# Two transformer blocks on one core: the modulation vectors as TensorE products in four column strips

## The chip, the cores and the metric

The kernel runs on 1 core of one Trainium2 chip. The metric is the device time of one execution in microseconds (us); less is better. The engines in the text: TensorE (PE; its weight loads are shown apart as PEld), VectorE (DVE), ScalarE (ACT), GpSimd (POOL), and SyncE (SP), whose queue issues nearly all transfers.

## What is computed

Two blocks for 256 tokens of width 1024, one after the other. The first mixes four branches (forgetting attention, a linear recurrence, stick-breaking attention, attention to a memory) and ends in a feed-forward part. The second has two layers, each applied to the tokens `x` and, in the first layer, also to 256 context tokens. All is fp32. What matters here are the modulation vectors of the second block:

```python
silu_c = jax.nn.silu(c)            # 1 x 1024
silu_cc = jax.nn.silu(c_ctx)       # 1024
for l in range(2):
    mod = silu_c @ w_ada[l] + b_ada[l]                 # w_ada[l]: 1024 x 6144
    sh1, sc1, g1, sh2, sc2, g2 = jnp.split(mod, 6)
    mod_c = silu_cc @ w_ada[l][:, :n_cm * 1024] + ...  # n_cm: 6 in layer 0, 2 in layer 1
```

They need nothing but `c`, `c_ctx` and the weights (two times 24 MB), so they can be made at any time before the second block's layer uses them.

## The kernel before

**Layout.** Activations lie feature-major: 8 tiles of 128 features x 256 tokens. Nearly every projection goes by *units*: a unit is 128 x 1024 weights (512 KB) that SP brings into `raw` (5 buffers; `unit`, L442). ACT rounds it to `whi` (L357), VectorE or GpSimd makes the rest `wlo = raw - whi` (L360), and TensorE makes 24 products of 128x128 weights and 256 columns from it (`mm3`, tiles `mm`: 8 of `hh` with `whi`, 8 of `hl` with `whi`, 8 of `hh` with `wlo`). Three PSUM buffers hold `mm`, four hold everything else (`ps`, tag `at`), one holds `st`.

**Order.** A scheduling layer orders the instructions of each engine by priority, and each engine then works strictly in that order. The program is written with generators that are stepped in turn (`step`, `run`, `weave`), so that side work is spread over a stage.

**The side work of this case** is `ada_steps` (L1053). For each layer it goes over 6 groups `g` of 1024 outputs, each in 4 steps of two 128-row slices of `w_ada`: 24 steps a layer, 48 in all. A step loads 1 MB into `wada` by SP (L1071), and VectorE multiplies each slice by the column of `silu(c)` (and of `silu(c_ctx)` where `nv` is 2) and adds it to `adacc`, 128 x 1024 for each vector (L367 the first time, L363 after that): 4 instructions a step with two vectors, 2 with one. Two steps after a group's last, `ada_end` (L1095) sums over the partitions: products of `adacc` with `sel`, a 128x32 matrix with one column of ones, four to a vector, each into its own strip of 32 partitions of one PSUM bank `ad`; ACT copies the bank to `adas`; two transposes on TensorE (L1106); VectorE adds the bias (tiles `ada`).

**Where it runs.** Layer 0 (`fill0`): 12 steps are written beside stick-breaking attention and the branch after it (`take(fill, 8)`, `take(fill, 4)` in `block1`), with one buffer for `wada`, and 12 beside the first block's feed-forward part (`ffn`, L1020), one to each of its pairs of units, with two buffers. Layer 1 (`fill1`): 12 beside the context's feed-forward part of layer 0, one to two pairs, and 12 beside that of the tokens, one to a pair; two buffers. `self.fp` names pool, tag, count of buffers and the tag of `adacc`.

**The feed-forward part of the first block** has, for each of 22 pairs of units, this chain: ACT copies the gate's half out of PSUM (`gp`), VectorE makes a three-tap convolution (`cv`: one L367, two L363), ACT the silu, VectorE the product with the other half (L360, which frees the PSUM buffer), ACT `hidh`, VectorE or GpSimd `hidl`. The second block's has no convolution.

Of the kernel before, what the change touches and what calls it, by code (L numbers as in the profile page):

```python
# [10 lines left out]
F32 = mybir.dt.float32  # L11
# [3 lines left out]
AF = mybir.ActivationFunctionType  # L15
ALU = mybir.AluOpType
AX = mybir.AxisListType

P = 128
D = 1024  # L20
T = 256
KT = 8
# [299 lines left out]
class Builder:  # L322
# [339 lines left out]
    def block1(self, xt, ct, fill):  # L662
        nc = self.nc
        with self.pool("b1") as bp, self.phase("b1t", t1=4, t2=6):
            def newy():
                return tuple(Tiles([bp.tile([P, T], F32R, tag="y" + c, name="y" + c, bufs=14) for _ in range(KT)])
                             for c in "hl")
            memt = bp.tile([P, KT, T], F32, tag="acc", name="memt")
            for i in range(0, KT, 2):
                nc.sync.dma_start(memt[:, i:i + 2], self.a["tok"][1, :, i:i + 2])  # L670
            late = PV["lam"][0]
            nc.sync.dma_start(self.pv[:, :late], self.a["pv"][:, :late])
            mh = newy()
            self.rms_h(memt, "mem_g", *mh)
            mk = bp.tile([P, KT, T], F32, tag="mk", name="mk")
            mv = bp.tile([P, 2, D], F32, tag="mv", name="mv")
            kv = self.mem_kv(mh, mk, mv)
            step(kv, 1)
            nc.sync.dma_start(xt, self.a["tok"][0])
            nc.sync.dma_start(self.pv[:, late:], self.a["pv"][:, late:])  # L680
            h = self.new_h()
            self.rms_h(xt, "attn_g", *h)
            self.setup()
            self.cb = bp.tile([P, NCB], F32, tag="cb", name="cb")
            nc.sync.dma_start(self.cb, self.a["cst1"])
            wr = self.t("wfr", P)
            nc.sync.dma_start(wr, self.a["wff"].rearrange("p k c -> p (k c)"))
            self.wff = [bp.tile([P, P], F32R, tag=f"wff{q}", name=f"wff{q}") for q in "hl"]
            self.split(wr, *self.wff, eng=nc.vector)
            run(kv)  # L690
            nc.sync.dma_start(ct, self.a["tok"][2])
            acc = bp.tile([P, KT, T], F32, tag="acc", name="acc")
            ym = newy()
            run(self.mem(h, mk, mv, ym))
            self.wl = bp.tile([P, 2, KT, P], F32, tag="mk", name="wl")
            nc.sync.dma_start(self.wl, self.a["wl"])
            gf = bp.tile([P, len(LEVELS), P], F32, tag="mv", name="gf")
            nc.sync.dma_start(gf, self.a["gm"])
            nc.vector.tensor_copy(self.gm, gf)
            yl = newy()  # L700
            lru = self.lru(h, yl, bp)
            step(lru, 1)
            b3 = self.branch(3, h, ym, acc, True)
            for _ in range(8):
                step(b3, 1)
                step(lru, 1)
            run(b3, lru)
            self.fp = bp, "mk", 1, "mv"
            self.span = 12
            yf = newy()  # L710
            fox = self.fox(h, yf, bp)
            step(fox, 3)
            weave((fox, 1), (self.branch(1, h, yl, acc, False), 1))
            ys = newy()
            stick = self.stick(h, ys, bp)
            step(stick, 3)
            bf = self.branch(0, h, yf, acc, False)
            weave((stick, 3), (bf, 1), (take(fill, 8), 1))
            run(bf)
            weave((self.branch(2, h, ys, acc, False), 2), (take(fill, 4), 1))  # L720
            mx = newy()
            self.halve(acc, mx)
            for f in range(0, KT, 2):
                self.residual(xt, self.pair("out", f, mx), f)
            h = self.new_h()
            self.rms_h(xt, "ffn_g", *h, True)
            self.flush()
        with self.pool("b1f") as bp, self.phase("b1ft", t1=10, t2=6):
            def hidden(ft, pg):
                gp = bp.tile([P, 2 + T], F32, tag="gp", name="gp", bufs=3)  # L730
                nc.gpsimd.memset(gp[:, :2], 0.0)
                self.act(gp[:, 2:], pg)
                c = self.t("cv")
                w = lambda i: self.pvc("fcw", i * FT + ft)
                self.ts(c, gp[:, 0:T], w(0), self.pvc("fcb", ft), ALU.mult, ALU.add)
                self.stt(c, gp[:, 1:1 + T], w(1), c, ALU.mult, ALU.add)
                self.stt(c, gp[:, 2:2 + T], w(2), c, ALU.mult, ALU.add)
                self.act(c, c, AF.Silu)
                return c

            self.fp = bp, "wada", 2, "adacc"
            self.span = 24
            yield from self.ffn("gu", "dn", h, hidden, lambda ps, f: self.residual(xt, ps, f), bp)

# [308 lines left out]
    def ada_steps(self, l, out):  # L1053


        nc = self.nc
        raws = []
        n = 0
        for g in range(6):
            nv = 2 if l == 0 or g < 2 else 1  # L1060
            for k in range(0, KT, 2):
                if self.late:
                    self.late[0] -= 1
                    if self.late[0] == 0:
                        self.flush()
                pool, rt, nr, at = self.fp
                if k == 0:
                    acc = pool.tile([P, 2, 1024], F32, tag=at, name="adacc")
                while len(raws) < nr and n < self.span:
                    raw = pool.tile([P, 2, 1024], F32, tag=rt, name="wada", bufs=nr)  # L1070
                    nc.sync.dma_start(raw, self.a["wa"][l * 24 + n])  # L1071
                    raws.append(raw)
                    n += 1
                raw = raws.pop(0)
                with self.tc.high_priority(offset=-200):
                    for j in range(2):
                        for v in range(nv):
                            c = self.sc[:, 2 * (k + j) + v:2 * (k + j) + v + 1]
                            if k + j == 0:
                                self.ts(acc[:, v], raw[:, j], c, None, ALU.mult)  # L1080
                            else:
                                self.stt(acc[:, v], raw[:, j], c, acc[:, v], ALU.mult, ALU.add)
                if k < KT - 2:
                    yield
            self.late = [2, lambda g=g, acc=acc, nv=nv: self.ada_end(l, out, g, acc, nv)]
            yield
        self.flush()

# [3 lines left out]
            f, self.late = self.late[1], None  # L1092
            f()

    def ada_end(self, l, out, g, acc, nv):  # L1095
        nc = self.nc
        ps = self.ps("ad")
        for v in range(nv):
            for j in range(4):
                self.mm(ps[j * 32:(j + 1) * 32, :T], self.sel[:, v], acc[:, v, j * T:(j + 1) * T], start=v == 0,  # L1100
                        stop=v == nv - 1)
        s = self.cp.tile([P, T], F32, tag="adas", name="adas")
        self.act(s, ps[:, :T])
        pt = ps[:, T:]
        for b in range(2):
            nc.tensor.transpose(pt[:, b * P:(b + 1) * P], s[:, b * P:(b + 1) * P], self.cst("ident"))  # L1106
        for v in range(nv):
            src = pt.rearrange("p (b j c) -> p j b c", b=2, j=4)[:, :, :, v]
            o = PV[f"bada{l}"][0] + g * 8
            self.tt(out[v][:, g * 8:(g + 1) * 8].rearrange("p (j b) -> p j b", b=2), src,  # L1110
                    self.pv[:, o:o + 8].rearrange("p (j b) -> p j b", b=2), ALU.add)
            if g in (1, 4):
                c = out[v][:, g * 8:(g + 1) * 8]
                self.ts(c, c, 1.0, None, ALU.add)
# [386 lines left out]
    def setup(self):  # L1501
        nc, cp = self.nc, self.cp
        nc.sync.dma_start(self.cc, self.a["cst"])
        c = lambda n, w: cp.tile([P, w], F32, tag=n, name=n)
# [21 lines left out]
        for l in range(2):  # L1526
            self.ts(self.pvs(f"dw{l}"), self.pvs(f"dw{l}"), 0.5, None, ALU.mult)

        self.sc = c("sc", 16)
        self.act(self.sc, self.pvs("c"), AF.Silu)  # L1530
        self.sel = cp.tile([P, 2, 32], F32, tag="sel", name="sel")
        nc.gpsimd.memset(self.sel, 0.0)
        for v in range(2):
            nc.gpsimd.memset(self.sel[:, v, v:v + 1], 1.0)


class Tiles:
# [14 lines left out]
def program(tc, a, out, stage, order):  # L1552
    nc = tc.nc
    with ExitStack() as ctx:
        b = Builder(tc, a, ctx, order)
# [21 lines left out]
            b.mix(0, nxt[0], xt, ax0, mem, bp, bp, b.modulate(ct, ac0, 3, nxt))  # L1577
        with b.pool("h2") as h2:
            with b.pool("f0") as bp, b.phase("f0t", t1=10, t2=6):
                b.fp = bp, "wada", 2, "adacc"  # L1580
                b.span = 24
                ffn = b.layer_ffn(0, nxt[1], ct, ac0, bp)
                for i in range(12):
# [2 lines left out]
                g = b.modulate(xt, ax0, 3, nxt)  # L1586
# [47 lines left out]
```

## Time and profile before

| what | value |
|---|---|
| median of 3 runs (lowest, highest) | 3097.9 us (3092.52 to 3099.93) |
| profiled execution, its own time | 3095.87 us |
| its span, first to last instruction | 3094.1 us |
| TensorE busy | 2809.3 us (91%) |
| VectorE busy | 2152.1 us (70%) |
| ScalarE, GpSimd busy | 1344.0 us, 851.9 us |
| mean granted TensorE clock | 0.961 |

Busy time is the union of an engine's instructions. An fp32 product on TensorE shows as two matmul records, a product of rounded (fp32r) operands as one. A granted clock of 1.0 is 2.4 GHz; the other level is 1.2 GHz, and values between are means over a stretch. What ended an engine's idle time (the releaser) is inferred from semaphores.

### The profile page before, as it was taken

To read this page: it belongs to the slowest core of one execution; us is meant where nothing else is said; L and a number is where in the kernel's file an instruction comes from. 1 tells how busy PE (TensorE), PEld (TensorE's weight loads), DVE (VectorE), ACT (ScalarE), POOL (GpSimd) and SP (SyncE) were. 2 spreads that over 40 slices of the span, in tenths; PEclk is the share of its full clock that TensorE was granted. 3 is DMA by queue.
4 is the path that set the end of the run, shared out by engine and by line. 5 is a ranking of instruction groups with operands and counts; after the bars stand their busy time and mean duration, and the time that the engine had idled before them with its cause. 6 is when DMAs were issued, how large, how long until landed. Compare 5 with 4: busy or idle time off the path is not lost. (4 is left out here: it accounts for less than half of the span.)

```text
span 3094.1 us, 49653 instructions
## 1 busy us (share of the span) xinstructions
PE 2809.3 (91%) x19760; PEld 2635.7 (85%) x19760; DVE 2152.1 (70%) x3412; ACT 1344.0 (43%) x2047; POOL 851.9 (28%) x643
## 2 busy tenths in 40 slices
PE   7997889988799887898999998999999999999898
PEld 6897778888799886798899988999998888888898
DVE  7599764679974899957699348868844499321554
ACT  5474446533344544345645554445434332111443
POOL 3243322243324434542102105444520111100000
PEclk9999999998899998999999999999999999999999
DMA  5345333466547555687656986654743223344353
GB/s 201 138 164 179 114 105 132 146 214 214 192 148 266 200 190 188 214 309 284 240 206 244 333 318 235 248 202 156 281 157 123 97 96 109 120 150 153 123 179 108
DMA packets 153416, 578.18 MB, mean 187 GB/s; under 512 B 17628, under 2 KB 17756, under 8 KB 146656
## 3 DMA queue, kind: packets, MB, share of 16 engines
q1 hardware_dynamic: 152496, 574.45, 52.1%
q8 instruction: 155, 2.54, 0.3%
q10 hardware_dynamic: 688, 0.56, 0.1%
q14 instruction: 77, 0.63, 0.1%
HBM read 516.73 MB, written 58.20 MB: 186 GB/s over the span
## 5 line engine op out<-in xcount | busy, mean ns | idle before, releaser
L357 ACT ACTIVATE whi<-raw 128x1024 fp32r<-128x1024 f32 (+1 forms) x650 | 675.7, 1045 | 747.4 <-PE mm L370 397.8
L360 POOL TENSOR_TENSOR wlo<-raw,whi 128x1024 fp32r<-128x1024 f32 (+1 forms) x248 | 647.0, 2613 | 1010.3 <-ACT whi L357 721.2
L360 DVE TENSOR_TENSOR wlo<-raw,whi 128x1024 fp32r<-128x1024 f32 (+1 forms) x293 | 382.8, 1307 | 242.3 <-ACT whi L357 231.0
L370 PE MATMUL mm<-hh,whi 128*128 128x256 f32 x3184 | 485.7, 294 | 33.1 <-DVE cv L360 19.2
L370 PE MATMUL mm<-hh,wlo 128*128 128x256 f32 x3184 | 469.3, 290 | 19.7 <-DVE wlo L360 17.6
L370 PE MATMUL mm<-hl,whi 128*128 128x256 f32 x3184 | 475.3, 292 | 0.0
L370 PEld LDWEIGHTS mm<-hh,whi 128*128 128x128 f32 x3184 | 431.2, 198 | 46.8 <-DVE cv L360 20.9
L370 PEld LDWEIGHTS mm<-hh,wlo 128*128 128x128 f32 x3184 | 426.0, 197 | 23.2 <-DVE wlo L360 18.8
L370 PEld LDWEIGHTS mm<-hl,whi 128*128 128x128 f32 x3184 | 431.7, 200 | 4.3 <-issue 3.6
L363 DVE SCALAR_TENSOR_TENSOR ca<-yp,pv,ca 128x256 f32<-128x256 f32 x720 | 357.2, 557 | 2.2
L370 PE MATMUL mm<-h,raw 128*128 128x256 f32 x1184 | 267.1, 379 | 0.0
L370 PEld LDWEIGHTS mm<-h,raw 128*128 128x128 f32 x1184 | 222.7, 190 | 29.5 <-issue 0.4
L363 DVE SCALAR_TENSOR_TENSOR adacc<-wada,sc,adacc 128x1024 f32<-128x1024 f32 x140 | 229.9, 1659 | 7.2 <-DMA wada<-in_wa 6.8
L360 POOL TENSOR_TENSOR gF<-cum 128x128 f32<-128x128 f32 x192 | 98.2, 542 | 337.2 <-DVE cum L1192 171.3
L370 PE MATMUL mm<-yh,whi 128*128 128x256 f32 x896 | 139.7, 295 | 23.1 <-ACT yh L357 16.3
L370 PEld LDWEIGHTS mm<-yh,whi 128*128 128x128 f32 x896 | 122.6, 199 | 30.1 <-ACT yh L357 20.6
L363 DVE SCALAR_TENSOR_TENSOR gt<-gt,mm 128x256 f32<-128x256 f32 x72 | 29.9, 416 | 161.7 <-ACT gt L357 161.6
L370 PE MATMUL mm<-yh,wlo 128*128 128x256 f32 x896 | 133.2, 290 | 2.8 <-DVE wlo L360 2.8
L370 PE MATMUL mm<-yl,whi 128*128 128x256 f32 x896 | 133.0, 290 | 2.6 <-DVE yl L363 2.1
L370 PEld LDWEIGHTS mm<-yh,wlo 128*128 128x128 f32 x896 | 120.0, 197 | 4.4 <-DVE wlo L360 3.2
L370 PEld LDWEIGHTS mm<-yl,whi 128*128 128x128 f32 x896 | 120.2, 197 | 3.6 <-DVE yl L363 2.7
L370 PE MATMUL mm<-y,raw 128*128 128x256 f32 x512 | 116.5, 384 | 0.0
(289 smaller groups left out, 4069.2 us busy)
## 6 DMA issues: line engine op xcount, KB each, us to landing
raw<-in_ws SPq DMA_DIRECT2D x744, 512.0 KB, 3.8
lo<-wlo SPq DMA_DIRECT2D x109, 512.0 KB, 3.0
wlo<-lo SPq DMA_DIRECT2D x109, 512.0 KB, 3.6
wada<-in_wa SPq DMA_DIRECT2D x48, 1024.0 KB, 4.9
raw<-in_ws SPq DMA_DIRECT2D x32, 384.0 KB, 3.0
memt<-in_tok SPq DMA_DIRECT2D x4, 256.0 KB, 4.6
xt<-in_tok SPq DMA_DIRECT2D x1, 1024.0 KB, 6.8
ct<-in_tok SPq DMA_DIRECT2D x1, 1024.0 KB
```

What stands on the lines that cost most here:

```text
L357: return self.nc.scalar.activation(out, in_, f, **k)
L360: return (eng or self.nc.vector).tensor_tensor(out=out, in0=a, in1=b, op=op)
L363: return self.nc.vector.scalar_tensor_tensor(out=out, in0=a, scalar=s, in1=b, op0=op0, op1=op1)
L370: return self.nc.tensor.matmul(out, lhsT=l, rhs=r, start=start, stop=stop, **k)
```

## The change

The products of a step are made on TensorE. `sc` becomes eight 128x32 matrices, one for each slice, with `silu(c)` and `silu(c_ctx)` in the first two columns and zeros in the others. Each step issues 8 products: for each of its two slices four, one to a strip of 32 partitions of the bank `ad`, with 256 columns of `wada` each. The bank is taken at a group's first step and accumulates over its 4 steps. `ada_end` no longer multiplies by `sel`; it starts at the copy to `adas` and comes one step after the group's last, not two. `adacc` and `sel` go, `wada` has three buffers instead of two in the feed-forward parts, and the lowered priority of the side work goes with the VectorE instructions.

```diff
-            self.fp = bp, "mk", 1, "mv"
+            self.fp = bp, "mk", 1
...
-            self.fp = bp, "wada", 2, "adacc"
+            self.fp = bp, "wada", 3
...
-                pool, rt, nr, at = self.fp
+                pool, rt, nr = self.fp
                 if k == 0:
-                    acc = pool.tile([P, 2, 1024], F32, tag=at, name="adacc")
+                    ps = self.ps("ad")
                 while len(raws) < nr and n < self.span:
...
-                with self.tc.high_priority(offset=-200):
-                    for j in range(2):
-                        for v in range(nv):
-                            c = self.sc[:, 2 * (k + j) + v:2 * (k + j) + v + 1]
-                            if k + j == 0:
-                                self.ts(acc[:, v], raw[:, j], c, None, ALU.mult)
-                            else:
-                                self.stt(acc[:, v], raw[:, j], c, acc[:, v], ALU.mult, ALU.add)
+                for j in range(2):
+                    for q in range(4):
+                        self.mm(ps[q * 32:(q + 1) * 32, :T], self.sc[:, k + j], raw[:, j, q * T:(q + 1) * T],
+                                start=k + j == 0, stop=k + j == KT - 1)
...
-            self.late = [2, lambda g=g, acc=acc, nv=nv: self.ada_end(l, out, g, acc, nv)]
+            self.late = [1, lambda g=g, ps=ps, nv=nv: self.ada_end(l, out, g, ps, nv)]
...
-    def ada_end(self, l, out, g, acc, nv):
+    def ada_end(self, l, out, g, ps, nv):
         nc = self.nc
-        ps = self.ps("ad")
-        for v in range(nv):
-            for j in range(4):
-                self.mm(ps[j * 32:(j + 1) * 32, :T], self.sel[:, v], acc[:, v, j * T:(j + 1) * T], start=v == 0,
-                        stop=v == nv - 1)
-        s = self.cp.tile([P, T], F32, tag="adas", name="adas")
+        s = self.t("adas")
         self.act(s, ps[:, :T])
...
-        self.sc = c("sc", 16)
-        self.act(self.sc, self.pvs("c"), AF.Silu)
-        self.sel = cp.tile([P, 2, 32], F32, tag="sel", name="sel")
-        nc.gpsimd.memset(self.sel, 0.0)
-        for v in range(2):
-            nc.gpsimd.memset(self.sel[:, v, v:v + 1], 1.0)
+        self.sc = cp.tile([P, KT, 32], F32, tag="sc", name="sc")
+        nc.gpsimd.memset(self.sc, 0.0)
+        self.act(self.sc[:, :, :2], self.pvs("c").rearrange("p (k v) -> p k v", v=2), AF.Silu)
```

**What moves, on VectorE, in the first block's feed-forward part** (`cv`, `hidl`, `wlo` are its own work; `adacc` the side work). Before, between two convolutions:

```order
L367 TENSOR_SCALAR cv<-gp,pv 128x256
L363 SCALAR_TENSOR_TENSOR adacc<-wada,sc,adacc 128x1024
L360 TENSOR_TENSOR wlo<-raw,whi 128x1024
L363 SCALAR_TENSOR_TENSOR cv<-gp,pv,cv 128x256
L363 SCALAR_TENSOR_TENSOR adacc<-wada,sc,adacc 128x1024
L363 SCALAR_TENSOR_TENSOR cv<-gp,pv,cv 128x256
L363 SCALAR_TENSOR_TENSOR adacc<-wada,sc,adacc 128x1024
L360 TENSOR_TENSOR cv<-cv,mm 128x256
L363 SCALAR_TENSOR_TENSOR adacc<-wada,sc,adacc 128x1024
```

Now:

```order
L367 TENSOR_SCALAR cv<-gp,pv 128x256
L363 SCALAR_TENSOR_TENSOR cv<-gp,pv,cv 128x256 x2
L360 TENSOR_TENSOR cv<-cv,mm 128x256
L360 TENSOR_TENSOR hidl<-cv,hidh 128x256
L360 TENSOR_TENSOR wlo<-raw,whi 128x1024
```

The side work is gone from between the steps of a pair's chain.

**On TensorE, in the same part, at the end of a group of the side work.** Before (`ad<-cc,adas` are the transposes):

```order
L370 MATMUL mm<-hh,wlo 128x256 x8
L370 MATMUL ad<-adacc,sel 32x256 x4
L370 MATMUL mm<-hh,whi 128x256 x8
L370 MATMUL mm<-hl,whi 128x256 x8
L370 MATMUL mm<-hh,wlo 128x256 x8
L370 MATMUL mm<-hh,whi 128x256
L370 MATMUL ad<-adacc,sel 32x256 x4
L370 MATMUL mm<-hh,whi 128x256 x5
L1106 MATMUL ad<-cc,adas 128x128 x2
```

Now:

```order
L370 MATMUL mm<-hh,wlo 128x256 x8
L370 MATMUL ad<-wada,sc 32x256 x5
L1099 MATMUL ad<-cc,adas 128x128 x2
L370 MATMUL ad<-wada,sc 32x256 x3
L370 MATMUL mm<-hh,whi 128x256 x8
```

Eight strip products stand after every pair of units, and the transposes of the group before stand inside the eight of the next step.

**On TensorE, beside stick-breaking attention** (`z` its logits, `av` its values), the first step of the side work now:

```order
L370 MATMUL z<-se,cb 128x256
L370 MATMUL z<-se,cb 128x128 x2
L370 MATMUL mm<-hh,whi 128x256 x4
L370 MATMUL mm<-hl,whi 128x256 x2
L370 MATMUL av<-sw,av 64x256
L370 MATMUL ad<-wada,sc 32x256
L370 MATMUL av<-sw,av 64x256
L370 MATMUL av<-sw,av 64x128 x2
L370 MATMUL ad<-wada,sc 32x256 x7
```

The first 12 steps now stand on TensorE here and in the branch after it. In the trace of before five of them ran on VectorE during the forgetting attention ahead of this stage, from 236 us on.

## Rows read from the trace of the kernel before

**Rows 1.** The page: busy time and share of the span by engine.

```profile
PE 2809.3 (91%) x19760; PEld 2635.7 (85%) x19760; DVE 2152.1 (70%) x3412; ACT 1344.0 (43%) x2047; POOL 851.9 (28%) x643
```

**Rows 2.** Groups of instructions: form xcount | busy us, mean ns | idle before, releaser.

```profile
L363 DVE SCALAR_TENSOR_TENSOR adacc<-wada,sc,adacc 128x1024 f32<-128x1024 f32 x140 | 229.9, 1659 | 7.2 <-DMA wada<-in_wa 6.8
...
L370 PE MATMUL ad<-adacc,sel 128*32 128x256 f32 x160 | 13.8, 443 | 10.5 <-DVE adacc L363 10.5
L370 PE MATMUL mm<-h,raw 128*128 128x256 f32 x1184 | 267.1, 379 | 0.0
```

**Rows 3.** Busy time by stretch: length, PE, PEld, DVE, ACT, POOL, PEclk, DMA share, GB/s.

```profile
576.00:696.00 120.00, 106.15 (x791) 97.41 (x790) 93.18 (x100) 51.29 (x74) 42.68 (x19) 0.91 0.55 195
696.00:873.00 177.00, 149.91 (x1105) 142.88 (x1106) 165.50 (x191) 68.82 (x115) 67.82 (x44) 0.88 0.54 192
1886.00:2040.00 154.00, 147.15 (x1178) 144.54 (x1179) 120.55 (x105) 62.54 (x91) 76.74 (x36) 0.95 0.67 242
2140.00:2230.00 90.00, 85.25 (x700) 83.33 (x699) 74.12 (x71) 41.96 (x68) 43.74 (x21) 0.96 0.68 249
```

**Rows 4.** Stretches, PE and PEld alone: length, PE, PEld, PEclk, DMA share, GB/s.

```profile
853.00:873.00 20.00, 20.00 (x169) 20.00 (x168) 1.00 0.35 127
1710.00:1752.00 42.00, 42.00 (x352) 42.00 (x351) 1.00 0.90 327
```

**Rows 5.** Stretch 696 to 873, adacc alone: length, PE, PEld, DVE, PEclk, DMA, GB/s.

```profile
696.00:873.00 177.00, 4.76 (x48) 1.13 (x48) 69.02 (x48) 0.88 0.54 192
```

**Rows 6.** Waits of PE, 696 to 873: total us, times, longest us.

```profile
PE mm L370 <- DVE cv L360: 13.9, 6, 3.8
PE ad L370 <- DVE adacc L363: 6.7, 3, 5.3
```

**Rows 7.** Timeline of PE around strip products: start us, us, instruction, xcount.

```profile
1941.30 1.12 PE L370 MATMUL mm<-hh,wlo 128*128 128x256 f32 x8
1942.35 1.07 PE L370 MATMUL ad<-adacc,sel 128*32 128x256 f32 x16
1943.35 0.98 PE L370 MATMUL mm<-hh,whi 128*128 128x256 f32 x6
...
1944.16 0.39 PE L1106 MATMUL ad<-cc,adas 128*128 128x128 f32 x2
```

**Rows 8.** Timeline of DVE behind the last adacc of that feed-forward part.

```profile
863.27 2.37 DVE L367 TENSOR_SCALAR cv<-gp,pv 128x256 f32<-128x256 f32 x1
...
869.65 2.44 DVE L367 TENSOR_SCALAR cv<-gp,pv 128x256 f32<-128x256 f32 x1
```

**Rows 9.** Waits of PE, 576 to 696.

```profile
PE mm L370 <- ACT yh L357: 4.1, 2, 2.9
PE ad L370 <- DVE adacc L363: 3.7, 1, 3.7
```

**Rows 10.** Waits of PE, 228 to 310, beside the forgetting attention.

```profile
PE pt L942 <- DVE fs L367: 3.7, 3, 1.8
```

**Rows 11.** Waits of PE, 873 to 930.

```profile
PE st L370 <- DVE fsum L566: 5.0, 1, 5.0
```

**Rows 12.** Waits of PE, 1886 to 2040.

```profile
PE mm L370 <- DVE hidl L360: 2.8, 1, 2.8
PE mm L370 <- DVE wlo L360: 2.2, 2, 1.9
```

**Rows 13.** Timeline of PE, the tokens' feed-forward part: in brackets idle before, releaser.

```profile
2190.11 0.64 PE L370 MATMUL ad<-adacc,sel 128*32 128x256 f32 x8
2190.68 0.74 PE L370 MATMUL mm<-hh,whi 128*128 128x256 f32 x4
2196.16 0.69 PE L1106 MATMUL ad<-cc,adas 128*128 128x128 f32 x2 [4.75 <-ACT adas L357]
```

**Rows 14.** Timeline of ACT ahead of the copy of that bank.

```profile
2194.51 1.06 ACT L357 ACTIVATE whi<-raw 128x1024 fp32r<-128x1024 f32 x1 [6.53 <-DMA raw<-in_ws]
...
2195.73 0.38 ACT L357 ACTIVATE adas<-ad 128x256 f32<-128x256 f32 x1
```

More of the change, by code (lines that the diff above doesn't have):

```diff
@@ L1579, in program @@
             with b.pool("f0") as bp, b.phase("f0t", t1=10, t2=6):
-                b.fp = bp, "wada", 2, "adacc"
+                b.fp = bp, "wada", 3
                 b.span = 24
```

## The prediction

> **What bounds the kernel now.** I read the page's table of engines first: the reader is to see TensorE at 91% of the span and VectorE at 70% [rows 1]. Over the whole program TensorE is the bound, so a change that adds products to it should cost. But a share of the span averages over stages, so next I read the stretches in which the side work runs [rows 3]. The feed-forward part of the first block, 696 to 873 us, stands out: VectorE is busy for 165.5 of its 177 us, TensorE for 149.9, and the granted TensorE clock is 0.88. There VectorE is the bound. In the other three stretches TensorE leads, with 106 of 120, 147 of 154 and 85 of 90 us. A granted clock of 0.88, if it is a mixture of the two levels 1.2 and 2.4 GHz, means that 24% of the stretch ran at 1.2, some 42 us, and half of these, 21 us, is what this costs.
>
> Third come the waits of TensorE in that stretch [rows 6]: 13.9 us for `cv`, the convolution's last product on VectorE, and 6.7 for `adacc`. Last I looked for a stretch in which TensorE does the same work without stalls: 853 to 873 us, behind the last of the side work, has 169 products in 20.00 us at clock 1.00 [rows 4], so 0.1183 us a product. What the stage would be without stalls can be worked out from that.
>
> **What the change removes.** VectorE loses 140 instructions of 1659 ns, 229.9 us [rows 2], and 20 lighter ones that begin a group; 69.0 us of these lie in 696 to 873 us [rows 5]. TensorE loses 80 products with `sel` (160 records), in 8 visits to the strips of 8 products and 4 of 4.
>
> **What it adds: the price of a step.** An fp32 product on the full array takes two records of 379 ns that overlap: 267.1 us for 592 products, 0.45 us each [rows 2]. In strips it is cheaper: 16 records, 8 products, start at 1942.35 us and the next work at 1943.35, so 1.00 us for eight [rows 7]; 8 records take 0.57 (2190.11 to 2190.68) [rows 13]. So four strips do four products in about the time of one on the whole array. Around a visit something is lost: the 8 products ahead take 1.05 us where eight take 0.96 elsewhere (853 to 873: 8 x 0.118 = 0.95), and the 6 behind 0.81 (1943.35 to 1944.16) where 0.72 is due [rows 4, 7], 0.09 on either side. A visit of 8 then costs 1.00 + 0.18, about 1.2 us, one of 4 about 0.76. The change has 48 visits of 8: 57.6 us, against 8 x 1.2 + 4 x 0.76 = 12.6 removed. TensorE gets 45 us of work more, and this has to be earned back from stalls.
>
> The Trainium skill, "TensorEngine Tiling (Array Packing)", section Key Properties, speaks against the change: switching the tiling mode drains the engine. The 0.09 us on either side of a visit agree with it; by these rows it is 48 x 0.18 = 9 of the 57.6 us.
>
> The Trainium skill, "TensorE: Matmul & The Clock Gate", section Measured speedup vs the span model, gives a speedup of 3.07 for four tiles at once, where 4 x 0.45 / 0.50 is 3.6 here. By 3.07 four products would take 0.59 us instead of 0.50, an estimate of 48 x 2 x 0.09 = 8 us more than in my sum; the row decides.
>
> **Stage by stage**, as gains (-) and costs (+):
>
> *Forgetting attention, 228 to 310 us.* Five steps' VectorE work leaves. TensorE's wait for `fs` on VectorE is 3.7 us [rows 10]; all of it could go: -4, bounds 0 and -7 (the whole wait and its low clock's share).
>
> *Stick-breaking attention and the branch after it, 576 to 696.* Twelve visits come in, 14.4 us, three go, 3.6: +10.8. The wait for `adacc`, 3.7 us, goes, and I give half of the 4.1 for `yh`, 2 us [rows 9]. The clock of 0.91 [rows 3] costs 11 us, from 18% of 120 at 1.2 GHz; products that fill idle time should win back half, 5. That is about 0. Bounds: -8 (all of these and the idle time) and +25. The upper one is a new wait: the bank `ad` is now held for four steps, so attention has three `at` banks in place of four, and might wait 2.9 us, the longest wait of the stage for `yh`, at each of five pairs of heads. I take the lower side, for the added products wait for `wada` alone.
>
> *First feed-forward part, 696 to 873.* 44 units of 24 products are 1056 x 0.1183 = 125 us [rows 4]. With the side work now in place of `adacc`: 125 + 12 x 1.2 + 0.5 for transposes = 140. Is VectorE's chain fast enough then? Behind the last `adacc` one convolution starts 6.4 us after the other (863.27, 869.65) [rows 8], while a pair of units takes TensorE 5.7 us and, with its step, 6.9. So TensorE becomes the bound again, by half a microsecond per pair. For what stays (the start, where the first units wait for their inputs and run at low clock) I add 10, a quarter of the 37 us by which the stage is longer now than 140: 150, that is -27. Bounds: -37 (no rest at all), and -9, where the wait for `cv` shrinks only by half and the clock stays low.
> Transfers must keep up: two units and a step are 2.1 MB per 6.9 us, 304 GB/s. Another stretch moves 327 GB/s with TensorE busy for all of its 42 us [rows 4], so this is covered; without this cover each pair would last as long as its transfers. The third `wada` buffer lets SP issue a step's load earlier, and a load queued behind it waits less.
>
> *Behind it, from 873.* TensorE waits 5.0 us for `fsum`, VectorE's sums that come late behind its backlog [rows 11]. The backlog goes: -5, bounds 0 and -7.
>
> *Context feed-forward of the second block, 1886 to 2040.* VectorE is no bound here (120.6 of 154 us [rows 3]), so the 14.4 us less 2.4 for removed visits mostly count. Back come the waits for `hidl` and `wlo`, 2.8 + 2.2 [rows 12], and 3 of the 8 us that a clock of 0.95 costs: +4, bounds 0 and +12.
>
> *Tokens' feed-forward, from 2140.* 14.4 - 4 x 0.76 = +11.4. The transposes wait 4.75 us there for `adas` [rows 13]; on ACT that copy stands behind a `whi` that waits 6.53 us for its transfer [rows 14]. SP had just been held at a step's load, which needs a `wada` buffer that VectorE reads; with three buffers and products in place of `adacc` I let this wait go, and with it half of the 3.6 us that the clock of 0.96 costs [rows 3]: +5, bounds +4 and +11.
>
> **Sum:** -4 + 0 - 27 - 5 + 4 + 5 = -27 against the profiled execution's 3095.9 us: 3068.9. The median of the runs is 2.0 above that execution, so I forecast 3070.
>
> **The rivals.**
> *The first feed-forward part stays bound by VectorE's chain (no change).* The chain of 6.4 us per pair is longer than the 5.7 of bare units [rows 8]; if ACT's and POOL's parts keep it there and the strips come at bad places, the waits for `cv` stay. For it: 13.9 us of them before, in only six waits. Against: with 69 us less VectorE has some 40% of the stage free. Then -4, +4, -9, -3, +8, +7, together +3: 3100.
>
> *ScalarE's copy becomes the wait (slower).* The transposes stand inside the next step's strips, so the copy of the bank to `adas` must be done five products behind the step's start; on ACT it stands behind other work, a `whi` that waits for its transfer in the worst case [rows 14]. If each of 12 ends waits as long as the worst seen, 4.75 us [rows 13], that is 57, less some 7 that such waits cost already: +50 on the forecast, 3120. It decides from 27 / 12 = 2.3 us a wait. Against: one pair of units, 5.7 us, lies between.
>
> *Every stall goes (a larger gain).* All lower bounds together, -7 - 8 - 37 - 7 + 0 + 4 = -55: 3041 to 3043. For it speaks that stalls breed low clock, which breeds stalls.
>
> *The strips don't overlap: the change doesn't do what it says.* Then 8 x 0.45 = 3.6 us a step in place of 1.0, 48 x 2.6 = +125: 3195. The rows of strips [rows 7, 13] speak against it, with the same shape and type.
>
> **How the numbers follow.** The forecast has 0.66, no change 0.14, the larger gain 0.12, the wait for `adas` 0.06, unoverlapped strips 0.02. The range goes down to the larger gain, 3041, and up to 3093, which takes in two of the upper bounds at once (first feed-forward at -9 in place of -27, and 5 more in the second block); beyond it lie the rivals without gain. Measurement of this kernel can tell about 0.3%, 9 us: faster is below 3088.6, slower above 3107.2. Faster has the forecast, less its upper tail, and the larger gain: 0.78; same 0.14; slower 0.08.
>
> **What would show it.** Right: `ad` products of 128x32 in 48 groups of about 1.0 us; in the first feed-forward part the clock near 0.95 or above, its length about 150 us, no long wait for `cv`, VectorE near 100 us busy; both feed-forward parts of the second block 4 to 5 us longer. Wrong: `cv` waits of several us as before; waits of products for an `at` bank beside stick-breaking attention; waits for `adas` at every group's end; visits of 2 us or more; SP waiting for `wada` with `raw` late behind it.

## The result and the profile after

The changed kernel takes 3062.9 us (median of 4 runs, 3057.5 to 3066.9) where the kernel before, run beside it, takes 3095.2: a ratio of 0.989 with a 95% interval of 0.987 to 0.991: 32 us less by the medians, some 34 by the ratio. Run again for the experiments it came out at 3063.3 and a ratio of 0.9891 (0.9877 to 0.9905). The forecast was 3070, the range 3041 to 3093.

The page of the kernel after, busy time by engine, to be held against [rows 1]:

```profile
PE 2834.0 (92%) x20368; PEld 2632.9 (86%) x20368; DVE 1924.1 (63%) x3252; ACT 1342.7 (44%) x2047; POOL 808.7 (26%) x641
```

TensorE does 25 us more and VectorE 228 us less, and the span is 29 us shorter in the profiled execution (3065.1 us). So TensorE's idle time and not its work shrank.

The strip products (all lines of the tile `ad` on TensorE; columns: instruction and count of records, shortest/median/longest ns, first and last start):

```profile
L370 PE MATMUL ad<-wada,sc x768: 379/379/637, 469.8 to 2214.2; 128*32 128x256 f32 x192
L1099 PE MATMUL ad<-cc,adas x24: 272/273/476, 544.3 to 2262.2; 128*128 128x128 f32 x24
```

They are there in full: 768 records, that is 384 products, 48 steps of 8. How they stand in the first feed-forward part, from TensorE's timeline of the kernel after:

```profile
760.54 1.12 PE L370 MATMUL mm<-hh,wlo 128*128 128x256 f32 x8
761.59 1.07 PE L370 MATMUL ad<-wada,sc 128*32 128x256 f32 x16
762.59 1.21 PE L370 MATMUL mm<-hh,whi 128*128 128x256 f32 x8
763.64 1.12 PE L370 MATMUL mm<-hl,whi 128*128 128x256 f32 x8
...
768.53 1.07 PE L370 MATMUL ad<-wada,sc 128*32 128x256 f32 x16
```

A visit of eight takes 1.00 us (761.59 to 762.59), the group ahead of it 1.05 and the one behind it 1.05 where 0.96 is the rule: 1.18 us in all, as summed. From one visit to the next, two units and a step, it is 6.94 us, without a gap.

**Where the time went.** To compare stage by stage I took instructions that both kernels have as marks, so that the same work lies between two marks: the products for `hsq` of the first query (`st`), the first transposes of `fs`, the first product of `z` from `se`, the first and last copy of a gate (`gp`), the first `hidh` of the second block, the last transposes of `adas`. The stretches between these marks, first of the kernel before, then of the kernel after (columns as in [rows 3]):

```profile
245.10:288.80 43.70, 35.00 (x242) 32.53 (x243) 41.94 (x44) 15.06 (x20) 16.49 (x8) 0.89 0.48 169
288.80:464.20 175.40, 148.15 (x1066) 132.69 (x1066) 122.79 (x215) 77.56 (x150) 49.37 (x24) 0.95 0.35 121
464.20:602.00 137.80, 131.25 (x979) 119.44 (x979) 65.72 (x94) 87.66 (x128) 39.12 (x16) 0.98 0.38 131
602.00:710.80 108.80, 95.83 (x700) 89.49 (x699) 86.56 (x95) 43.37 (x65) 39.31 (x20) 0.89 0.60 213
710.80:875.50 164.70, 140.45 (x1070) 134.63 (x1070) 153.59 (x174) 65.81 (x111) 64.69 (x40) 0.91 0.53 189
875.50:899.40 23.90, 18.32 (x133) 17.70 (x132) 22.14 (x28) 10.70 (x15) 4.95 (x3) 0.86 0.38 129
...
1886.10:2292.90 406.80, 386.81 (x3115) 380.16 (x3116) 302.85 (x294) 176.12 (x255) 192.48 (x103) 0.97 0.61 219
```

```profile
245.80:277.20 31.40, 24.18 (x166) 22.67 (x166) 25.45 (x31) 11.03 (x15) 9.48 (x6) 0.84 0.36 129
277.20:453.80 176.60, 157.77 (x1144) 141.76 (x1142) 117.88 (x213) 81.51 (x155) 52.55 (x26) 0.97 0.34 116
453.80:586.10 132.30, 129.53 (x1024) 114.74 (x1024) 52.85 (x84) 85.74 (x124) 36.53 (x15) 1.00 0.48 170
586.10:692.80 106.70, 102.16 (x831) 91.22 (x830) 44.11 (x68) 45.42 (x67) 36.78 (x21) 0.97 0.64 233
692.80:833.50 140.70, 135.42 (x1170) 126.14 (x1169) 112.43 (x131) 63.97 (x109) 53.06 (x40) 1.00 0.58 208
833.50:857.60 24.10, 20.10 (x128) 19.19 (x129) 21.75 (x28) 10.30 (x16) 4.13 (x2) 0.79 0.36 120
...
1850.20:2262.10 411.90, 402.84 (x3430) 381.30 (x3431) 194.33 (x226) 177.70 (x255) 171.10 (x103) 0.99 0.61 216
```

| stage | before, us | after, us | difference | forecast |
|---|---|---|---|---|
| forgetting attention (245 to 464) | 219.1 | 208.0 | -11.1 | -4 |
| stick-breaking attention, branch (to the first gate copy) | 246.6 | 239.0 | -7.6 | 0 |
| first feed-forward part, first to last gate copy | 164.7 | 140.7 | -24.0 | -27 |
| behind it, to the second block's first `ht` | 23.9 | 24.1 | +0.2 | -5 |
| feed-forward parts of the second block | 406.8 | 411.9 | +5.1 | +9 |

The sum of the table is -37; the rest of the program, in which nothing changed, is 8 us longer in this execution than in that of before. That is scatter: between the last gate copy and the first `hidh` of the second block lie 1010.6 us of the kernel before, and 1010.9 to 1018.6 in nine other profiles of this study, two of them of the changed kernel, with 1016.7 and 1016.8. A difference of a few us of one stage is therefore not settled by one pair of traces; for this there are the timed experiments.

In the first feed-forward part TensorE's idle time fell by 19 us (24.3 to 5.3) and its busy time by 5, though eight strip products a step came in: the granted clock rose from 0.91 to 1.00.

The waits that were to go, by TensorE's waits of the kernel after between 692.8 and 833.5 us. Of the rows for `cv` and `adacc` in [rows 6] nothing is left; this is the whole list:

```profile
PE mm L370 <- ACT whi L357: 1.2, 3, 0.4
PE ad L1099 <- ACT adas L357: 0.8, 1, 0.8
```

### The profile page after: what moved, and what is told of

It is laid out like the page before. It is cut to its first block, busy times and chain, and to the rows that moved or that the text cites. A ratio compares the mean times of both kernels' runs of the same rounds, so it can differ in the third digit from the quotient of the medians.

```text
span 3065.1 us, 50685 instructions
## 1 busy us (share of the span) xinstructions
PE 2834.0 (92%) x20368; PEld 2632.9 (86%) x20368; DVE 1924.1 (63%) x3252; ACT 1342.7 (44%) x2047; POOL 808.7 (26%) x641
## 4 chain that ended last, share of the span: by engine, by line
PE 45%; DVE 18%; ACT 3%; DMA 3%; issue 2%; POOL 1%; SPq 0%; DVEq 0%; ACTq 0%; POOLq 0%
PE mm L370 38%; DVE ca L363 7%; DMA raw<-in_ws 3%; PE st L370 2%; DVE gF L360 2%; PE av L370 1%; PE ga L370 1%; DVE wlo L360 1%; PE ad L370 1%; ACT whi L357 1%; DVE ht L363 1%; DVE sq L360 1%; POOL wlo L360 1%; DVE nr L363 1%; DVE fsum L566 1%
## 5 line engine op out<-in xcount | busy, mean ns | idle before, releaser
L360 POOL TENSOR_TENSOR wlo<-raw,whi 128x1024 fp32r<-128x1024 f32 (+1 forms) x248 | 613.1, 2474 | 1014.2 <-ACT whi L357 845.3
L360 DVE TENSOR_TENSOR wlo<-raw,whi 128x1024 fp32r<-128x1024 f32 (+1 forms) x293 | 372.4, 1272 | 334.0 <-ACT whi L357 317.1
L370 PE MATMUL mm<-hh,whi 128*128 128x256 f32 x3184 | 477.0, 291 | 17.5 <-ACT hh L357 5.6
L370 PE MATMUL mm<-hl,whi 128*128 128x256 f32 x3184 | 464.4, 288 | 0.0
L370 PEld LDWEIGHTS mm<-hh,whi 128*128 128x128 f32 x3184 | 422.4, 195 | 41.3 <-issue 8.8
L370 PEld LDWEIGHTS mm<-hl,whi 128*128 128x128 f32 x3184 | 421.3, 195 | 3.8 <-issue 3.1
L370 PEld LDWEIGHTS mm<-y,raw 128*128 128x128 f32 x512 | 98.0, 192 | 13.5
```

What stands on the lines that cost most here:

```text
L360: return (eng or self.nc.vector).tensor_tensor(out=out, in0=a, in1=b, op=op)
L370: return self.nc.tensor.matmul(out, lhsT=l, rhs=r, start=start, stop=stop, **k)
```

## Experiments

**Which stage pays, by itself.** Four kernels choose for each half of a layer's steps between TensorE's and VectorE's way: the first 12 steps (beside attention), the next 12 (beside the first feed-forward part), and the 24 of the second block. The buffers are those of the kernel whose way is taken.

```diff
-                for j in range(2):
-                    for q in range(4):
-                        self.mm(ps[q * 32:(q + 1) * 32, :T], self.sc[:, k + j], raw[:, j, q * T:(q + 1) * T],
-                                start=k + j == 0, stop=k + j == KT - 1)
+                if (l, g // 3) in ON_PE:
+                    ...
+                else:
+                    with self.tc.high_priority(offset=-200):
+                        ...
```

*TensorE only in the first feed-forward part* (`ON_PE = [(0, 1)]`):

> TensorE products only in the 12 steps beside the first block's feed-forward part; the other 36 steps on VectorE as before. Theory (each stage pays or gains by itself): this stage alone carries the gain that the trace of the changed kernel shows between its first and last gate copy, 164.7 to 140.7 us, so -24 us against the kernel before (3095 to 3071). Rival (the gain of this stage came from stages ahead of it that left VectorE without a backlog): -10 us or less here.

3073.9 us against 3098.1, ratio 0.9920 (0.9902 to 0.9938): -25 us, with -19 to -30 as the interval. The rival falls: this stage gains what the traces showed, though the stages ahead of it are those of the kernel before. Its rows are nearly those of the changed kernel:

```profile
712.00:851.90 139.90, 138.38 (x1212) 129.26 (x1210) 112.32 (x131) 64.39 (x110) 53.13 (x40) 1.00 0.61 216
```

*TensorE only in the first 12 steps* (`ON_PE = [(0, 0)]`):

> TensorE products only in the first 12 steps, beside the forgetting attention, stick-breaking attention and the branch after it. Theory: VectorE's 26 us in the forgetting attention delayed the keys kz, whose transfer TensorE then waited for; without them the stages up to the feed-forward part are 18 us shorter, as between the two traces (first gate copy at 710.8 and 692.8 us): -18 us. Rival (my forecast's figure for these stages, where only the waits for fs, adacc and half of yh go): -4 us.

3081.0 us, ratio 0.9943 (0.9927 to 0.9960): -18 us, -12 to -23. The -4 of my forecast lies outside. The run times two stages together; how the 18 us divide between them is read from the traces alone. What happens in the forgetting attention is seen on three engines. TensorE's first wait for the transfer of `kz` is about as long in both kernels, 6.74 us before and 7.20 after; in its timeline before, then after:

```profile
280.53 1.62 PE L370 MATMUL lg<-kz,qz 128*128 128x128 f32 x4 [6.74 <-DMA kz<-ncf]
```

```profile
271.77 1.62 PE L370 MATMUL lg<-kz,qz 128*128 128x128 f32 x4 [7.20 <-DMA kz<-ncf]
```

The wait is as long, but it ends 8.8 us sooner. ACT issues that transfer once `kz` is written on VectorE; the last link, VectorE's and ACT's timelines, before and after:

```profile
276.16 1.42 DVE L363 SCALAR_TENSOR_TENSOR kz<-hraw,pv,nr 128x512 f32<-128x512 f32 x2
...
276.94 2.79 ACTq L915 DMA_DIRECT2D kz<-ncf  x4
```

```profile
267.98 1.41 DVE L363 SCALAR_TENSOR_TENSOR kz<-hraw,pv,nr 128x512 f32<-128x512 f32 x2
...
268.76 2.52 ACTq L915 DMA_DIRECT2D kz<-ncf  x4
```

VectorE's chain of small steps to `kz` had `adacc` instructions of 1.3 to 3.4 us between them; without these `kz` is 8.2 us earlier. The row of the wait names the transfer, which is the last link and takes its time in either kernel; that VectorE was late behind it stands in no row of waits. The steps' loads leave this stretch too, and no run separates them from the VectorE work; but in the kernel before VectorE went without a wait from 243.8 us until `kz` was written, so no transfer held it up.

The products that TensorE did before the wait in the kernel before, it does after it now: 166 records in place of 242 in the first stretch, 1144 in place of 1066 in the second. There they can fill the later waits for `kz`, and it is these that shrink. The view of the tile `kz` has TensorE's idle time until that transfer, all heads together (us, times), before and after:

```profile
  DMA kz<-ncf: 25.0, 4
```

```profile
  DMA kz<-ncf: 13.2, 3
```

In the kernel with TensorE in these 12 steps alone it is 13.4 us, in the one with TensorE in the second block alone 25.2.

*TensorE only in the second block* (`ON_PE = [(1, 0), (1, 1)]`):

> TensorE products only in the 24 steps of the second block, where TensorE is the bound. Theory: 24 x 1.2 us less 5.4 us of sums over partitions is +23 us of TensorE work; stalls of about 18 us give most of it back: +5 us against before, as between the traces (35.9 us ahead at the first hidh, 30.8 at the last transposes). Rival (all of the added work counts): +20 us.

3103.0 us, ratio 1.0015 (1.0003 to 1.0026): +5 us, +1 to +8. As the traces had it. The waits for `hidl`, `wlo` and `adas` in [rows 12, 13] are gone, and the added products cost a little more than they did.

*TensorE only in the first block* (`ON_PE = [(0, 0), (0, 1)]`):

> TensorE products in the first block, VectorE in the second. Theory: the gain of the first block without the loss in the second: 5 us less than the changed kernel, 3058 where that has 3063; -37 us against before. Rival: no better than the changed kernel, since VectorE's stalls in the second block cost what the added products cost.

3052.0 us, ratio 0.9846 (0.9827 to 0.9864): -48 us. The three parts add up: -25 - 18 + 5 = -38 for the changed kernel (measured -34), -43 for this one. The sign of each part is shown; the last 5 us of this one are within the intervals.

**What a step costs TensorE.** Four kernels change the products of a step; all of them are the changed kernel otherwise. In the first each product is made twice, with all eight in a row:

```diff
                 for j in range(2):
-                    for q in range(4):
-                        self.mm(ps[q * 32:(q + 1) * 32, :T], ..., start=k + j == 0, stop=k + j == KT - 1)
+                    for r in range(2):
+                        for q in range(4):
+                            self.mm(ps[q * 32:(q + 1) * 32, :T], ..., start=k + j == 0 and r == 0, stop=...)
```

> Each strip product of the changed kernel is made twice, so the modulation vectors come out doubled. It prices the eight products of a step without a further change of tiling mode. Theory (eight products cost 1.00 us and lie on the path that sets the end in nearly every step): 44 to 48 us more than the changed kernel, 3107 to 3111. Rival (a good part of them fills idle time of TensorE): under 30 us more.

3107.1 us, ratio 1.0040 (1.0025 to 1.0055), 44 us above the changed kernel. TensorE's timeline of it has the price of the second eight:

```profile
788.00 1.93 PE L370 MATMUL ad<-wada,sc 128*32 128x256 f32 x32
789.86 1.22 PE L370 MATMUL mm<-hh,whi 128*128 128x256 f32 x8
```

Sixteen products take 1.86 us, so the second eight 0.86; 48 x 0.86 is 41 us, and 44 were paid. On the whole, then, nothing covers the second eight. That holds beside attention too: there the first gate copy comes at 705.3 us in place of 692.8, 12.5 us for 12 steps.

In the next the eight products of a step all go to one strip (the four steps of a group to the four strips in turn), which takes away only that strips work side by side:

```diff
-                        self.mm(ps[q * 32:(q + 1) * 32, :T], self.sc[:, k + j], raw[:, j, q * T:(q + 1) * T],
-                                start=k + j == 0, stop=k + j == KT - 1)
+                        o = k // 2 * 32
+                        self.mm(ps[o:o + 32, :T], self.sc[:, k + j], raw[:, j, q * T:(q + 1) * T],
+                                start=j + q == 0, stop=j + q == 4)
```

> All eight products of a step go into one strip, the four steps of a group into the four strips in turn; so a step has as many products of the same shape, and no other mode, but no two strips at work (the vectors come out wrong, the parts of 256 columns are added up). Theory (the strips' overlap makes 0.125 us of 0.45): 8 x 0.45 = 3.6 us a step for 1.0, 48 x 2.6 = 125 us more than the changed kernel, 3188. Rival (a product with 32 columns of weights is short by itself): no more than 10 us more.

3176.9 us, ratio 1.0247 (1.0229 to 1.0266): 114 us above the changed kernel. TensorE's timeline:

```profile
799.67 3.19 PE L370 MATMUL ad<-wada,sc 128*32 128x256 f32 x14
802.78 1.22 PE L370 MATMUL mm<-hh,whi 128*128 128x256 f32 x8
```

The window begins behind the first of the eight. Seven products take 3.11 us, 0.444 each, the 0.45 of a product on the full array [rows 2]. The short time of the strips is their overlap and nothing else. Without it the change would be a loss of 78 us.

In the last two, seven full-array products of 16 columns are added to each step, once between its eight and once behind them, written to the other half of the bank (in these two the modulation vectors come out changed):

```diff
+                        if j * 4 + q < 7:
+                            self.mm(ps[:, T:T + 16], self.cst("ident"), raw[:, 0, :16], skip_group_check=True)
```

> The same seven full-array products of 16 columns behind the eight strip products of each step. About 0.18 us each, by the transposes of 128 columns (two in 0.39 us): 48 x 7 x 0.18 = 60 us more than the changed kernel, 3123.

> Seven full-array products of 16 columns are put between the eight strip products of each step (into the unused half of the bank, which the transposes overwrite). Against the kernel with the same seven behind the eight. Theory (a change of tiling mode costs 0.18 us for both sides, and strips separated by another product do not overlap): seven more pairs of changes, 1.3 us, and eight products at 0.45 in place of 1.0 in all, 2.6 us: 3.9 us a step, up to 180 us more than with the seven behind. Rival (only the change of mode counts, or only the overlap is lost): 60 or 125 us more. Rival (neither): the same time.

Behind the eight: 3140.7 us, ratio 1.0149 (1.0134 to 1.0164), 78 above the changed kernel and more than the 60 expected, since such a product takes 0.23 us, not 0.18. Between them: 3334.2 us, ratio 1.0787 (1.0767 to 1.0807), 193 us more for the same products in another order. TensorE's timelines, behind and then between:

```profile
795.67 1.07 PE L370 MATMUL ad<-wada,sc 128*32 128x256 f32 x16
796.67 1.74 PE L370 MATMUL ad<-wada,cc 128*128 128x16 f32 x14
798.26 1.19 PE L370 MATMUL mm<-hh,whi 128*128 128x256 f32 x8
799.29 1.12 PE L370 MATMUL mm<-hl,whi 128*128 128x256 f32 x8
```

```profile
796.95 0.62 PE L370 MATMUL ad<-wada,sc 128*32 128x256 f32 x2
797.50 0.39 PE L370 MATMUL ad<-wada,cc 128*128 128x16 f32 x2
797.83 0.62 PE L370 MATMUL ad<-wada,sc 128*32 128x256 f32 x2
...
803.62 1.21 PE L370 MATMUL mm<-hh,whi 128*128 128x256 f32 x8
```

Behind, a step takes 2.59 us (1.00 and 1.59); between, 6.67 (796.95 to 803.62). The difference of 4.08 us x 48 is 196, and 193 were measured. Both of the named costs are there: a strip product that stands alone takes 0.55 us, 0.45 and 0.10 for the change to it, and the ordinary one behind it 0.33, 0.23 and 0.10 for the change back. So of 4.1 us a step 2.6 are lost overlap (8 x 0.45 less 1.0) and 1.5 are changes. The Trainium skill, "TensorEngine Tiling (Array Packing)", section Key Properties, has such a drain at a change of tiling mode; these rows agree, with 0.10 us a change, though they do not separate the mode from the change of weights that comes with it. And a border can cost without a change of mode: behind the seven full-array products the next eight ordinary ones take 1.03 us (798.26 to 799.29) where 0.96 is the rule. What differs there is fp32 against rounded operands and the columns, so a good part of the 0.09 that I put down to the mode behind a visit may be that.

**What lay beside the products.** The end of the last group stood in the program behind 22 pairs of units, though its products are done after 12:

```diff
-        step(ffn, 10)
-        run(fill0)
+        step(ffn, 2)
+        run(fill0)
+        step(ffn, 8)
```

> The changed kernel, with the end of the first layer's last group (copy to adas, transposes) written eight pairs of units earlier. Theory (the 5 us that I expected behind the feed-forward part went into the 4.0 us wait for adas): that wait goes, 4 us less than the changed kernel. Rival (VectorE's fsum is late by its own place in the program, so that TensorE waits for it instead, as the 6.8 us in the kernel with TensorE in the first block alone): the wait for fsum grows from 1.3 to 5 us or more, and no time is gained.

3062.7 us, ratio 0.9887 (0.9873 to 0.9901), against 3063.3 of the changed kernel beside it: no gain. TensorE's waits from 825 to 866 us, first of the changed kernel in the same series, then of this one:

```profile
PE ad L1099 <- ACT adas L357: 4.0, 1, 4.0
PE st L370 <- DVE sq L360: 1.5, 1, 1.5
PE st L370 <- DVE fsum L566: 1.3, 1, 1.3
```

```profile
PE st L370 <- DVE fsum L566: 6.5, 1, 6.5
PE st L370 <- DVE sq L360: 1.5, 1, 1.5
```

The wait for `adas` only stood in front of the one for `fsum`. With it gone TensorE arrives sooner and waits longer for the same thing, 6.5 us in place of 4.0 + 1.3. The rival is right: `fsum` on VectorE starts 3.1 us behind the last gate copy in the kernel before and 2.5 us behind it in the changed one and in this one, and takes 3.6 to 3.7 us in each.

The third `wada` buffer, taken back in the feed-forward parts:

```diff
-            self.fp = bp, "wada", 3
+            self.fp = bp, "wada", 2
...
-                b.fp = bp, "wada", 3
+                b.fp = bp, "wada", 2
```

> The changed kernel with two wada buffers in the feed-forward parts, as before the change. Theory (the third buffer is no part of the gain, since the products that free a buffer take 1 us): within 3 us of the changed kernel. Rival (it is what keeps SP's queue free for the weights, above all in the first feed-forward part): 10 us or more of the gain is lost.

3063.0 us, ratio 0.9887 (0.9873 to 0.9901): the same as the changed kernel. The third buffer is no part of the gain.

The changed kernel itself, beside these:

> The changed kernel once more, beside the next three on one chip, so that they can be compared with it: 32 to 35 us less than before, a ratio of 0.989.

3063.3 us, ratio 0.9891 (0.9877 to 0.9905), as above. And what the parts point to, TensorE in the first block with the earlier end and VectorE in the second:

> TensorE in the first block with the earlier end of the last group, VectorE in the second block. Theory: 5 us less than the changed kernel from the second block, and what the earlier end gives; 5 to 9 us less. By the ratios of the earlier runs, 0.9846 against 0.989: 13 us less. Rival: the same as the changed kernel.

3054.7 us, ratio 0.9858 (0.9840 to 0.9877): some 9 us less than the changed kernel beside it. The two intervals just meet, so of itself this is likely and not certain; with the kernel that has TensorE in the first block alone (0.9846) it is the second one to come out below. The profiles point to the second block, with ranges that just overlap: the stretch from the first `hidh` of the second block to the last transposes is 400.4 to 410.2 us long in the five kernels that use VectorE there (406.8 before), and 409.4 to 414.7 in the five that use TensorE (411.9 in the changed one).

## Why the prediction was right, and where it was not

- **The bound of the first feed-forward part.** Right. VectorE was it; with 12 steps on TensorE the stage ran at clock 1.00 and 135.4 of 140.7 us busy. The forecast was -27, the traces show -24.0 between the gate copies, and the stage alone gave -25 in the timed runs. The waits for `cv` did not stay (the rival of no change). One thing in it was only half right, that TensorE becomes the bound throughout. With a step a pair takes 6.94 us; but the last ten pairs, without side work, start their convolutions 6.4 us apart (795.50, 801.95, 808.39 us in VectorE's timeline) where bare units take 5.76, and TensorE's three waits for `whi` stand there. So there the chain of [rows 8] sets the pace; which engine makes it 6.4 us long is not shown.
- **The price of a step.** Right to some hundredths: 1.00 us and 0.18 around it. A step and a pair of units were put at 6.9 us and take 6.94. That all of it counts in time was assumed, and the doubled products showed it for a second eight.
- **Overlap of strips.** The rival without it was put at 3.6 us a step and +125 us; a kernel without overlap pays 114 (111 by the ratios).
- **The forgetting attention: the term that was mis-sized**, -4 with bounds 0 and -7, where the traces have -11.1. The failed step is "TensorE's wait for `fs` on VectorE is 3.7 us", with "all of it could go" as its value. I priced the wait that names VectorE [rows 10], and not those for `kz`, whose row names a transfer. That transfer was released by VectorE, 8.2 us late at the first of them, and over the stage these waits fell from 25.0 to 13.2 us; those for `fs` stayed, 9.2 and 8.9. The bounds were taken from the row of `fs` and so did not hold the value. It was also four steps that left this stage, 16 `adacc` instructions of 26 us, and not five.
- **Stick-breaking attention and the branch**, put at 0, measured -7.6, inside the bounds of -8 and +25 but at their end. TensorE's busy time rose by only 4.6 us over the two stretches (131.25 + 95.83 to 129.53 + 102.16), where +10.8 was summed, since the clock rose from 0.98 and 0.89 to 1.00 and 0.97. Half of the clock's loss was my guess, and more came back. Idle time fell by 12.2 us (19.5 to 7.3). That idle time would have covered added products anyway is not shown: a second eight cost its full price here. The list of TensorE's waits in the two stretches now has no wait for an `at` bank, which I feared, nor for `yh` and `adacc`, but a new one for a step's load:

```profile
PE ad L370 <- DMA wada<-in_wa: 3.3, 2, 2.4
PE av L370 <- ACT sw L357: 1.4, 3, 0.5
PE z L370 <- DVE se L360: 1.3, 1, 1.3
PE ad L1099 <- ACT adas L357: 1.1, 1, 1.1
```

- **Behind the feed-forward part**, put at -5, measured +0.2. The failed step is "The backlog goes": the wait for `fsum` was not VectorE's backlog. In the kernel with 36 steps still on VectorE and none here the wait is 6.8 us, and an earlier end of the last group moves it back to 6.5.
- **Second block**, put at +9, measured +5.1, and +5 (1 to 8) by itself. TensorE's busy time rose by 16 us, where 23 were summed, and its idle time fell by 11. The third `wada` buffer, to which I gave a part in this, has none: two serve as well.
- **The rival that is slower**, waits for `adas` at each end: three of 12 ends wait, 5.9 us in all, less than the 6.8 before. At the other nine ends one pair of units was enough time for ScalarE's copy, and 4.0 of the 5.9 us stand in front of the wait for `fsum`, where their going gained nothing.

In sum the forecast missed by 7 us. Two terms ahead of the first feed-forward part were too small by 15 together, and one behind it was too large by 5. Part of the closeness is luck: the five rows of the table miss by -10 in all, and the 8 us by which the rest of the program was longer offset most of that in the profiled execution. The forecast of "faster" rested on the right stage.

## What to carry to other kernels

Before work is moved from one engine to another, look stage by stage at which of the two ends last: here the same 1.18 us a step bought about 25 us beside a stage bound by VectorE, and cost 5 in stages bound by TensorE, and the kernel that uses each engine where the other is the bound came out below both pure ones, some 9 us below the better of them with intervals that just meet. A wait that names a transfer must be followed to what released the transfer; the engine that is late may be one link further back, and the idle time that it costs may show at a later wait. Products with few columns of weights belong next to each other, strip by strip: eight of them with seven ordinary ones took 2.59 us apart and 6.67 us interleaved.

## What was not expected of the hardware

Going from a full-array product to a strip product and back has a price of its own beyond the lost overlap, 0.10 us each way (0.55 us for a strip product alone where 0.444 is the time of one in a row in one strip). Strips overlap as good as fully: eight products took 1.00 us where 8 x 0.45 is 3.6, a factor of 3.6, and a second eight in the same visit 0.86 us, 0.11 a product against 0.444, a factor of 4.1. The Trainium skill, "TensorE: Matmul & The Clock Gate", section Measured speedup vs the span model, has 3.07 for four row tiles at once (K=32, N=512), and for column strips a row with three tiles only; so its figure is a neighbour's. The measurement is higher here, and decides.
